# Where the norm weights are applied: on the features or on the weight matrices

## The chip, the cores and the metric

One core of one Trainium2 chip. The metric is the device time in microseconds (us) of one execution. The kernel before was timed three times: 1508.42, 1510.27 and 1512.3 us, median 1510.27.

## What is computed

A sequence of 256 rows of width 1024 goes through two blocks in fp32. What matters here is that every projection is preceded by a norm with a weight vector `g`, and that the product is linear in both:

```python
def rmsnorm(x, g):
    xf = x.astype(jnp.float32)
    y = xf * lax.rsqrt(jnp.mean(xf * xf, axis=-1, keepdims=True) + NORM_EPS)
    return y.astype(x.dtype) * g
...
    for l in range(DEPTH):
        g = norm_gains[l]
        h = rmsnorm(x, g[0])
        if l % 2 == 0:
            y = even_mixer(h, ...)
        else:
            y = odd_mixer(h, ...)
        x = x + rmsnorm(y, g[1])
        h = rmsnorm(x, g[2])
        x = x + rmsnorm(memory_cross_attention(h, mem_n, w_q[l], w_kv[l], w_o[l]), g[3])
        h = rmsnorm(x, g[4])
        x = x + rmsnorm(squared_relu_mlp(h, w_ff1[l], w_ff2[l]), g[5])
```

The second block is a differential attention, an MLP, an S5 state space layer (`ssm`) and an MLP, each behind a norm with its own weights; the attention's heads go through another norm (`subln`) before `w_o`. Per layer of the first block there are a mixer (pooling and a gated recurrence in layer 0, banded attention in layer 1), attention to a normed memory `mem`, and an MLP. The MLPs are 1024 to 4096 to 1024.

## The kernel before

Every fp32 product is made as three matmuls of fp32r parts: each operand is split into a high part (a rounded copy) and a low part (the value less the high part), and hi x hi, hi x lo and lo x hi are summed. The rows stand in two tiles of 128 (`X`, t = 0 and 1). The row factor of a norm is applied after the product, the weight vector `g` before it.

*Activations.* `feat_half` (L133 to L144) transposes four 128x128 blocks of `X` on TensorE (L140) into one PSUM tile `tp`, copies it to `hh` on ACT (L143) and makes `hl` = tp - hh on DVE (L144), 128x512 each. Two halves make one row tile's features. `residual` (L178) puts these calls into a list, `later`, that `now` (L206) runs in the midst of the next product. `mem_feat` (L407) does the same once for the memory (`mh`, `ml`), after a sum of squares on ACT (L416) and a scaling on DVE (L421).

*Weights.* A `Seg` (L25) is a panel of a weight matrix. `_load` (L34) fetches 512 KB at a time into a `raw` buffer (four of them) by a transfer that SP issues (L42), ACT makes `whi`, DVE `wlo` (rings of ten). One `raw` holds one k tile of 128x1024, or two of 128x512. Where a weight vector belongs to the rows of the matrix, its column of `gcols` (or `sg`, for `subln`) is the scale, k tile by k tile:

```python
            if self.gain is None:
                nc.scalar.activation(out=hi, in_=src, func=AF.Copy)                       # L47
                ...
            else:
                for a, kt in enumerate(kts):
                    g = self.gain[:, kt:kt + 1]
                    nc.scalar.activation(out=hi[:, a], in_=src[:, a], func=AF.Copy, scale=g)  # L53
                    ...
                        nc.vector.scalar_tensor_tensor(out=lo[:, a], in0=src[:, a], scalar=g, ...)  # L58
```

*Products.* `proj_b` (L259) has the weights stationary and gives feature-major results (`pb`, 128x256 matmuls, L224 to L226), `proj_a` (L242) the activations stationary (`pacc`, `acc`, 128x512, L217 to L219). `mlp` (L275) works in eight chunks of 512 hidden columns, `ffps` and `ffacc`. The second layer's MLP of the first block and the first MLP of the second block also run `tables` between their matmuls, a generator that makes the S5 layer's tables: `er`, `gr`, `cmt`, `bb` on DVE (L1149 to L1157, L1376), `bm` partly on GpSimd, transposes `etp` on TensorE (L1402) and copies `eo` and `kl` on ACT (L1403, L1416). `diff` (L628) is the differential attention.

*Order.* A scheduler fixes the order of the instructions on each engine when the program is built; each engine then runs its list strictly in that order. In `even` (L858) a block under `manual_schedule` (L889) makes the first features and the first panel. SP issues the transfers in its own list: `X`, `gcols` (L1825), the first weights, some small tables, `mem` (L413).

Of the kernel before, what the change touches and what calls it, by code (L numbers as in the profile page):

```python
# [24 lines left out]
class Seg:  # L25


    def __init__(self, c, dram, c0, width, kts, gain=None, share=False):
# [4 lines left out]

    def _load(self, i):  # L34
# [5 lines left out]
        for j in range(2):  # L40
# [5 lines left out]
            if self.gain is None:  # L46
                nc.scalar.activation(out=hi, in_=src, func=AF.Copy)  # L47
                eng = nc.gpsimd if self.share and j else nc.vector
                eng.tensor_tensor(out=lo, in0=src, in1=hi.bitcast(F32), op=ALU.subtract)  # L49
# [19 lines left out]
class Core:  # L69
# [108 lines left out]
    def residual(self, t, acc, gain=None, rsq=None, feat=True, rows=True):  # L178
# [16 lines left out]
        for q in range(2):  # L195
# [1685 lines left out]
```

## Time and profile before

| what | value |
|---|---|
| median of three runs | 1510.27 us |
| the profiled execution | 1508.71 us |
| its span from the first instruction to the last | 1506.9 us |
| TensorE (PE) busy | 1426.2 us, 95% |
| VectorE (DVE) busy | 1129.7 us, 75% |
| ScalarE (ACT) busy | 835.0 us, 55% |
| GpSimd (POOL) busy | 184.0 us, 12% |
| DMA, mean | 198 GB/s |

The profile is one execution. Its views used here: groups of instructions by line (how often, how long), waits (who stood still, for whom), busy time by stretch of the span, and the timeline. A wait is idle time of an engine that ended with the named event. Idle time of an engine that nobody waits for costs nothing. `PEclk` is TensorE's granted clock as a share of its full speed.

### The profile page before, as it was taken

What the parts mean: (1) busy time and instruction counts of PE and PEld (TensorE: products, weight loads), DVE (VectorE), ACT (ScalarE), POOL (GpSimd) and SP (SyncE); (2) the same over time, 40 slices, a digit from 0 to 9 for tenths busy, and PEclk for the clock granted to TensorE, in tenths of its full rate; (3) what the DMA queues carried; (4) which work ended last, traced back from release to release, by engine and by line L of the source; (5) the groups of instructions that cost most, each with busy time, mean ns of one, the idle gap of its engine ahead of it and who ended that gap; (6) DMA issues with size and microseconds to landing.
All of it is one profiled execution on the core that took longest, in us unless ns stands there. A gap on an engine that the chain in (4) does not pass through costs nothing. (4 is left out here: it accounts for less than half of the span.)

```text
span 1506.9 us, 25499 instructions
## 1 busy us (share of the span) xinstructions
PE 1426.2 (95%) x9668; PEld 1239.6 (82%) x9668; DVE 1129.7 (75%) x2013; ACT 835.0 (55%) x1432; POOL 184.0 (12%) x206
## 2 busy tenths in 40 slices
PE   8999999999999999989899999999999968999997
PEld 8897888998789798869778877888879756889895
DVE  7986658997776866579995699899995587674651
ACT  7475546454464665556445667665454555564540
POOL 1241001000000000023440010123430000000000
PEclk9999999999999999999999999999999998999999
DMA  8464535475785455365768663347668887655640
GB/s 298 145 206 155 188 119 188 152 238 181 241 284 188 127 182 194 114 210 191 232 211 255 210 219 114 111 146 235 220 223 265 319 315 274 198 184 192 206 158 28
DMA packets 134034, 298.26 MB, mean 198 GB/s; under 512 B 16152, under 2 KB 36376, under 8 KB 133272
## 3 DMA queue, kind: packets, MB, share of 16 engines
q1 hardware_dynamic: 133624, 294.54, 58.9%
q0 software_dynamic: 288, 2.10, 0.4%
q8 instruction: 76, 1.25, 0.3%
q14 instruction: 46, 0.38, 0.1%
HBM read 270.15 MB, written 31.62 MB: 200 GB/s over the span
## 5 line engine op out<-in xcount | busy, mean ns | idle before, releaser
L58 DVE SCALAR_TENSOR_TENSOR wlo<-raw,gcols,whi 128x512 fp32r<-128x512 f32 (+1 forms) x456 | 356.7, 825 | 66.5 <-ACT whi L53 66.3
L53 ACT ACTIVATE whi<-raw,gcols 128x512 fp32r<-128x512 f32 (+1 forms) x456 | 316.7, 745 | 128.0 <-DMA raw<-in_w_ff 27.4
L49 DVE TENSOR_TENSOR wlo<-raw,whi 128x1024 fp32r<-128x1024 f32 x172 | 206.7, 1220 | 65.1 <-ACT whi L47 64.6
L47 ACT ACTIVATE whi<-raw 128x1024 fp32r<-128x1024 f32 x176 | 181.8, 1054 | 99.1 <-DMA raw<-in_ffn_w_down 28.6
L224 PE MATMUL ffps<-hh,whi 128*128 128x256 f32 x768 | 222.0, 289 | 0.2 <-ACT kl L1416 0.2
L226 PE MATMUL ffps<-hl,whi 128*128 128x256 f32 x768 | 219.6, 286 | 0.0
L225 PE MATMUL ffps<-hh,wlo 128*128 128x256 f32 x768 | 219.4, 286 | 0.0
L217 PE MATMUL ffacc<-whi,ah 128*128 128x512 f32 x512 | 206.1, 403 | 2.3 <-ACT whi L47 2.3
L218 PE MATMUL ffacc<-wlo,ah 128*128 128x512 f32 x512 | 203.5, 397 | 0.7 <-DVE wlo L49 0.7
L219 PE MATMUL ffacc<-whi,al 128*128 128x512 f32 x512 | 203.4, 397 | 0.0
L224 PEld LDWEIGHTS ffps<-hh,whi 128*128 128x128 f32 x768 | 148.2, 193 | 2.4 <-issue 1.4
L225 PEld LDWEIGHTS ffps<-hh,wlo 128*128 128x128 f32 x768 | 147.8, 192 | 0.5
L226 PEld LDWEIGHTS ffps<-hl,whi 128*128 128x128 f32 x768 | 147.6, 192 | 0.0
L217 PEld LDWEIGHTS ffacc<-whi,ah 128*128 128x128 f32 x512 | 97.3, 190 | 25.5 <-ACT whi L47 2.7
L218 PEld LDWEIGHTS ffacc<-wlo,ah 128*128 128x128 f32 x512 | 97.5, 190 | 22.7 <-DVE wlo L49 1.6
L219 PEld LDWEIGHTS ffacc<-whi,al 128*128 128x128 f32 x512 | 97.2, 190 | 23.0
L225 PE MATMUL pb<-hh,wlo 128*128 128x256 f32 x352 | 101.1, 289 | 2.9 <-DVE wlo L58 2.9
L224 PE MATMUL pb<-hh,whi 128*128 128x256 f32 x352 | 101.3, 290 | 2.2 <-ACT whi L53 2.2
L226 PE MATMUL pb<-hl,whi 128*128 128x256 f32 x352 | 100.8, 287 | 0.0
L171 POOL TENSOR_TENSOR r<-r,mhalf 128x1 f32<-128x1 f32 x32 | 24.7, 771 | 563.9 <-DVE r L170 557.2
L299 DVE TENSOR_TENSOR relu<-relu 128x512 f32<-128x512 f32 x64 | 45.7, 714 | 58.2 <-ACT relu L298 58.0
L298 ACT ACTIVATE relu<-ffps 128x512 f32<-128x512 f32 x64 | 43.9, 685 | 76.0 <-PE ffps L226 61.6
(481 smaller groups left out, 3001.7 us busy)
## 6 DMA issues: line engine op xcount, KB each, us to landing
raw<-in_w_ff SPq DMA_DIRECT2D x128, 512.0 KB, 4.6
raw<-in_ffn_w_up SPq DMA_DIRECT2D x64, 512.0 KB, 4.5
raw<-in_ffn_w_down SPq DMA_DIRECT2D x64, 512.0 KB, 4.4
raw<-in_w_mem_kv SPq DMA_DIRECT2D x32, 512.0 KB, 4.8
raw<-in_w_qkv SPq DMA_DIRECT2D x24, 512.0 KB, 4.9
raw<-in_attn_w_qkv SPq DMA_DIRECT2D x24, 512.0 KB, 4.7
raw<-in_w_in_ab SPq DMA_DIRECT2D x20, 512.0 KB, 5.1
raw<-in_w_mem_q SPq DMA_DIRECT2D x16, 512.0 KB, 5.1
```

What stands on the lines that cost most here:

```text
L47: nc.scalar.activation(out=hi, in_=src, func=AF.Copy)
L49: eng.tensor_tensor(out=lo, in0=src, in1=hi.bitcast(F32), op=ALU.subtract)
L53: nc.scalar.activation(out=hi[:, a], in_=src[:, a], func=AF.Copy, scale=g)
L58: nc.vector.scalar_tensor_tensor(out=lo[:, a], in0=src[:, a], scalar=g, in1=hi[:, a].bitcast(F32), op0=ALU.mult, op1=ALU.subtract)
L217: nc.tensor.matmul(o, xh, wh[:, s], start=first, stop=False)
L218: nc.tensor.matmul(o, xh, wl[:, s], start=False, stop=False)
L219: nc.tensor.matmul(o, xl, wh[:, s], start=False, stop=last)
L224: nc.tensor.matmul(out, wh, xh, start=first, stop=False)
L225: nc.tensor.matmul(out, wl, xh, start=False, stop=False)
L226: nc.tensor.matmul(out, wh, xl, start=False, stop=last)
L298: nc.scalar.activation(out=o, in_=ps if view is None else ps.rearrange("p (f c j) -> p f c j", f=2, j=8), func=AF.Relu)
L299: nc.vector.tensor_tensor(out=r, in0=r, in1=r, op=ALU.mult)
```

## The change

The vectors scale the activations. `feat_half` takes a `gain`: with a matrix of columns (128x8), each of its four 128x128 blocks has its own scale, so the ACT copy and the DVE subtraction are made block by block; with one column (128x1, `sg`) they stay 128x512. The 40 halves that go into normed products (36 `hh`, 4 `mh`) become four and four operations; the 4 halves of `diff`'s `o` keep one and one. All weights are split unscaled, one 128x1024 operation on ACT and one on DVE for each raw, except the first two raws of the first panel (`fine=1`), which stay in 128x512 pieces. The counts of transfers and of matmuls are the same. Matrices that had a gain: 244 raws, 212 of them in two 128x512 pieces, 32 in one 128x1024; 8 more of `w_o` had `sg`.

```diff
@@ class Seg, _load
-            if self.gain is None:
-                nc.scalar.activation(out=hi, in_=src, func=AF.Copy)
-                eng = nc.gpsimd if self.share and j else nc.vector
-                eng.tensor_tensor(out=lo, in0=src, in1=hi.bitcast(F32), op=ALU.subtract)
-            else:
-                for a, kt in enumerate(kts):
-                    g = self.gain[:, kt:kt + 1]
-                    nc.scalar.activation(out=hi[:, a], in_=src[:, a], func=AF.Copy, scale=g)
...
-                        nc.vector.scalar_tensor_tensor(out=lo[:, a], in0=src[:, a], scalar=g, in1=hi[:, a].bitcast(F32),
-                                                       op0=ALU.mult, op1=ALU.subtract)
+            eng = nc.gpsimd if self.share and j else nc.vector
+            for s in [slice(a, a + 1) for a in range(h)] if i < self.fine else [slice(0, h)]:
+                nc.scalar.activation(out=hi[:, s], in_=src[:, s], func=AF.Copy)
+                eng.tensor_tensor(out=lo[:, s], in0=src[:, s], in1=hi[:, s].bitcast(F32), op=ALU.subtract)
@@ feat_half
-        h = hi[:, ks, :]
-        nc.scalar.activation(out=h, in_=t3, func=AF.Copy)
-        nc.vector.tensor_tensor(out=lo[:, ks, :], in0=t3, in1=h.bitcast(F32), op=ALU.subtract)
+        h, l = hi[:, ks, :], lo[:, ks, :]
+        for s in (slice(0, 4),) if gain.shape[1] == 1 else (slice(j, j + 1) for j in range(4)):
+            g = gain if gain.shape[1] == 1 else gain[:, 4 * q + s.start:4 * q + s.stop]
+            nc.scalar.activation(out=h[:, s], in_=t3[:, s], func=AF.Copy, scale=g)
+            nc.vector.scalar_tensor_tensor(out=l[:, s], in0=t3[:, s], scalar=g, in1=h[:, s].bitcast(F32), op0=ALU.mult, op1=ALU.subtract)
@@ even
-                self.to_feat(self.X[:, t], hh[:, t], hl[:, t])
-            proj(1024, decay)
+                self.to_feat(self.X[:, t], hh[:, t], hl[:, t], gain)
+            proj(1024, decay, 1)
@@ residual: the next norm's columns come in as feat
-                self.later.append(lambda q=q: self.feat_half(X, q, self.hh[:, t], self.hl[:, t]))
+                self.later.append(lambda q=q: self.feat_half(X, q, self.hh[:, t], self.hl[:, t], gain=feat))
```

The other lines hand the columns to `residual`, `mem_feat` and `ssm` in place of the products, and make `sg` 128x1.

The scheduler orders the changed instructions anew. Three places, as the order of the two programs prints them. First ACT at the start: the features of `X` (`hh`), the first weights (`whi`), the memory's sum of squares (`ml,mms<-mem`). Before:

```order
L143 ACTIVATE hh_88<-tp_138 128x512
L143 ACTIVATE hh_88<-tp_145 128x512
L53 ACTIVATE whi_155<-raw_153,gcols_109 128x512 x2
L53 ACTIVATE whi_163<-raw_161,gcols_109 128x512 x2
L53 ACTIVATE whi_183<-raw_181,gcols_109 128x512 x2
L53 ACTIVATE whi_191<-raw_189,gcols_109 128x512 x2
L168 ACTIVATE junk_233,ms_234<-X_90 128x512 x2
```

After (the first seven slices of `hh` stand ahead of these rows):

```order
L899 ACTIVATE lbe_335<-lbe_335 128x4
L137 ACTIVATE hh_88<-tp_137,gcols_109 128x128
L137 ACTIVATE hh_88<-tp_150,gcols_109 128x128 x3
L410 ACTIVATE ml_115,mms_642<-mem_638 128x1024
L137 ACTIVATE hh_88<-tp_150,gcols_109 128x128
L137 ACTIVATE hh_88<-tp_163,gcols_109 128x128 x4
L49 ACTIVATE whi_179<-raw_177 128x512 x2
L49 ACTIVATE whi_187<-raw_185 128x512 x2
L49 ACTIVATE whi_207<-raw_205 128x1024
L49 ACTIVATE whi_213<-raw_211 128x1024
```

The sum of squares of the memory and the recurrence's `lbe` stand now ahead of the first weight split; the sum of squares stood behind sixteen of them before. In the list of SP, which is not printed, the second gain vector `gB`, `d_rows`, `g_rows` and two more small tables now come right behind the first half of `mem`, ahead of the fifth weight transfer; DVE multiplies `d_rows` by `g_rows` two slices before its first weight split.

Second, DVE in the even mixer, between the first panels' splits (`wlo`), the decay chain (`x`, `lx`, `f`, and `b`, the scan) and the memory's scaling (`mem`). Before:

```order
L939 SCALAR_TENSOR_TENSOR x_119<-x_119,lx_340 128x1024
L938 TENSOR_TENSOR f_342<-f_342,ls_352 128x1024
L874 TENSOR_TENSOR u0_360<-pb_444,rb_121 128x2x256
L943 SCALAR_TENSOR_TENSOR b_358<-reset_327,f_342 128x1024
L58 SCALAR_TENSOR_TENSOR wlo_534<-raw_531,gcols_109,whi_533 128x512 x2
L421 TENSOR_SCALAR mem_634<-mem_634,r_643 128x512
```

After:

```order
L922 SCALAR_TENSOR_TENSOR lx<-x 128x1024
L868 TENSOR_TENSOR u_380<-pb,rb 128x2x256
L415 TENSOR_SCALAR mem<-mem,r 128x512 x4
L50 TENSOR_TENSOR wlo<-raw,whi 128x1024
L931 SCALAR_TENSOR_TENSOR ls<-x,lx 128x1024
L933 SCALAR_TENSOR_TENSOR x<-x,lx 128x1024
L932 TENSOR_TENSOR f<-f,ls 128x1024
L868 TENSOR_TENSOR u_380<-pb,rb 128x2x256
L937 SCALAR_TENSOR_TENSOR b<-reset,f 128x1024
L960 TENSOR_TENSOR w<-u_380 128x4x256
L50 TENSOR_TENSOR wlo<-raw,whi 128x1024
```

Before, the last two pieces of the third panel stood behind the scan; now all splits of the first three panels stand ahead of these rows (two of them just ahead of `x`), the memory's scaling and one further split go before the chain.

Third, DVE in a chunk of the first table stage: four `wlo` of the second MLP matrix have been made (the last of them is the first L49 or L50 row), then the next chunk's first matrix. Before:

```order
L49 TENSOR_TENSOR wlo<-raw,whi 128x1024
L1376 TENSOR_TENSOR bb<-bb,gb 128x128
L49 TENSOR_TENSOR wlo<-raw,whi 128x1024
L58 SCALAR_TENSOR_TENSOR wlo<-raw,gcols,whi 128x512
L1151 TENSOR_TENSOR er<-pk,bb 128x512
L1152 TENSOR_TENSOR er<-pk,bb 128x512
L1153 TENSOR_TENSOR er<-er,cmt 128x512
L1157 TENSOR_TENSOR er<-er,cmt_8104 128x512
L58 SCALAR_TENSOR_TENSOR wlo<-raw,gcols,whi 128x512
L1151 TENSOR_TENSOR gr<-pk,bc 128x4x128
L1417 SCALAR_TENSOR_TENSOR kl<-dmask,d_rows,kl 128x16
```

After:

```order
L50 TENSOR_TENSOR wlo<-raw,whi 128x1024
L1370 TENSOR_TENSOR bb<-bb,gb 128x128
L50 TENSOR_TENSOR wlo<-raw,whi 128x1024
L1145 TENSOR_TENSOR er<-pk,bb 128x512
L1146 TENSOR_TENSOR er<-pk,bb 128x512
L1147 TENSOR_TENSOR er<-er,cmt 128x512
L1151 TENSOR_TENSOR er<-er,cmt_8052 128x512
L50 TENSOR_TENSOR wlo<-raw,whi 128x1024 x2
L1411 SCALAR_TENSOR_TENSOR kl<-dmask,d_rows,kl 128x16
L1145 TENSOR_TENSOR gr<-pk,bc 128x4x128
L1146 TENSOR_TENSOR gr<-pk,bc 128x4x128
L1147 TENSOR_TENSOR gr<-gr,cmt 128x4x128
```

The first two raws' `wlo` stand together behind the four `er` operations, one operation for each; before, the first piece stood ahead of them and the second behind.

## Rows read from the trace of the kernel before

**Rows 1.** The page's part 1: busy us, share of the span, instructions.

```profile
PE 1426.2 (95%) x9668; PEld 1239.6 (82%) x9668; DVE 1129.7 (75%) x2013; ACT 835.0 (55%) x1432; POOL 184.0 (12%) x206
```

**Rows 2.** Groups by line and shape, whole span (line, tiles, count | busy, mean ns | idle).

```profile
L58 DVE SCALAR_TENSOR_TENSOR wlo<-raw,gcols,whi 128x512 fp32r<-128x512 f32 x424 | 313.9, 784 | 59.1 <-ACT whi L53 58.9
L53 ACT ACTIVATE whi<-raw,gcols 128x512 fp32r<-128x512 f32 x424 | 280.8, 715 | 114.5 <-DMA raw<-in_w_ff 27.4 <-DMA raw<-in_ffn_w_up 23.6 <-PE ffacc L219 12.3
L49 DVE TENSOR_TENSOR wlo<-raw,whi 128x1024 fp32r<-128x1024 f32 x172 | 206.7, 1220 | 65.1 <-ACT whi L47 64.6
L47 ACT ACTIVATE whi<-raw 128x1024 fp32r<-128x1024 f32 x176 | 181.8, 1054 | 99.1 <-DMA raw<-in_ffn_w_down 28.6 <-DMA raw<-in_w_ff 27.8 <-PE pb L226 20.6
L144 DVE TENSOR_TENSOR hl<-tp,hh 128x512 fp32r<-128x512 f32 x36 | 23.4, 683 | 2.2 <-ACT hh L143 2.2
L143 ACT ACTIVATE hh<-tp 128x512 fp32r<-128x512 f32 x36 | 19.6, 586 | 4.2 <-PE tp L140 4.1
L1416 ACT ACTIVATE kl<-klag 128x144 f32<-128x144 f32 x16 | 4.3, 270 | 0.0
```

**Rows 3.** Busy time by stretch: engines (instructions), PEclk, DMA share, GB/s.

```profile
690.00:800.00 110.00, 100.22 (x813) 87.15 (x815) 105.35 (x166) 59.46 (x105) 39.73 (x36) 0.95 0.68 225
870.00:980.00 110.00, 105.05 (x565) 84.10 (x563) 101.74 (x245) 77.41 (x161) 11.61 (x8) 1.00 0.45 145
880.00:890.00 10.00, 10.00 (x45) 8.04 (x44) 10.00 (x11) 6.96 (x12) 2.96 (x1) 1.00 0.64 215
1025.00:1135.00 110.00, 103.51 (x839) 91.11 (x837) 103.92 (x164) 57.75 (x111) 40.59 (x38) 0.97 0.67 224
```

**Rows 4.** Waits, 690 to 800 us (first three), then 1025 to 1135 us.

```profile
PE etp L1402 <- ACT eo L1403: 5.6, 2, 3.3
ACT whi L53 <- DMA raw<-in_w_ff: 17.4, 4, 5.9
DVE wlo L58 <- ACT whi L53: 2.2, 4, 0.8
...
DVE wlo L58 <- ACT whi L53: 3.0, 6, 0.8
```

**Rows 5.** Timeline, runs of equal operations (start, us, engine, line, xcount).

```profile
321.10 2.73 DVE L58 SCALAR_TENSOR_TENSOR wlo<-raw,gcols,whi 128x512 fp32r<-128x512 f32 x4
324.49 2.35 DVE L49 TENSOR_TENSOR wlo<-raw,whi 128x1024 fp32r<-128x1024 f32 x2
331.95 1.41 DVE L58 SCALAR_TENSOR_TENSOR wlo<-raw,gcols,whi 128x512 fp32r<-128x512 f32 x2
...
318.60 2.55 ACT L53 ACTIVATE whi<-raw,gcols 128x512 fp32r<-128x512 f32 x4
321.54 2.00 ACT L47 ACTIVATE whi<-raw 128x1024 fp32r<-128x1024 f32 x2
330.32 1.34 ACT L53 ACTIVATE whi<-raw,gcols 128x512 fp32r<-128x512 f32 x2 [0.88 <-DMA raw<-in_w_ff]
...
123.52 1.12 DVE L1107 SCALAR_TENSOR_TENSOR y<-o,r,og 128x128 f32<-128x128 f32 x4 [0.91 <-POOL r L123]
...
L1107 DVE SCALAR_TENSOR_TENSOR y<-o,r,og x8: 341/343/351, 123.5 to 133.0; 128x128 f32<-128x128 f32 x8
```

**Rows 6.** The start: timeline of ACT, PE and SP, and tile mem.

```profile
7.67 0.60 ACT L143 ACTIVATE hh<-tp 128x512 fp32r<-128x512 f32 x1 [0.35 <-PE tp L140]
9.09 5.32 ACT L53 ACTIVATE whi<-raw,gcols 128x512 fp32r<-128x512 f32 x8 [0.82 <-DMA raw<-in_w_in_ab]
...
9.86 0.79 PE L224 MATMUL pb<-hh,whi 128*128 128x256 f32 x2 [2.23 <-ACT whi L53]
...
10.36 0.33 SPq L413 DMA_DIRECT2D mem<-in_mem  x1
...
L416 ACT ACTIVATE ml<-mem x2: 1047/1050/1052, 24.4 to 25.7; 128x1024 fp32r<-128x1024 f32 x2
DMA to landing us min/median/max: 6.4/6.4/6.4
...
raw<-in_w_in_ab SPq DMA_DIRECT2D x20, 512.0 KB, 5.1
```

**Rows 7.** Timeline at 38 to 42 us, and busy time by stretch.

```profile
37.98 2.28 DVE L943 TENSOR_TENSOR_SCAN b<-reset,f 128x1024 f32<-128x1024 f32 x1
40.17 2.17 DVE L58 SCALAR_TENSOR_TENSOR wlo<-raw,gcols,whi 128x512 fp32r<-128x512 f32 x2
...
40.95 0.58 PE L225 MATMUL pb<-hh,wlo 128*128 128x256 f32 x1 [2.86 <-DVE wlo L58]
...
20.00:30.00 10.00, 10.00 (x87) 10.00 (x86) 9.66 (x20) 9.79 (x19) 0.56 (x1) 1.00 0.84 285
40.00:50.00 10.00, 9.05 (x52) 8.96 (x53) 10.00 (x13) 3.83 (x4) 5.22 (x5) 0.66 0.18 53
70.00:120.00 50.00, 50.00 (x361) 46.87 (x360) 40.63 (x50) 37.81 (x61) 20.56 (x10) 1.00 0.60 200
```

**Rows 8.** Timeline of DVE in the first table stage; its splits, 690 to 800 us.

```profile
750.60 0.68 DVE L1151 TENSOR_TENSOR er<-pk,bb 128x512 f32<-128x512 f32 x1
754.48 1.55 DVE L1151 TENSOR_TENSOR gr<-pk,bc 128x512 f32<-128x512 f32 x1
...
L58 DVE SCALAR_TENSOR_TENSOR wlo<-raw,gcols,whi 128x512 fp32r<-128x512 f32 x32 | 29.0, 949 | 2.2 <-ACT whi L53 2.2
```

**Rows 9.** Waits, 870 to 980 us.

```profile
PE acc L217 <- ACT hh L143: 0.3, 1, 0.3
```

More of the change, by code (lines that the diff above doesn't have):

```diff
@@ L176, in row_scale, with residual @@
         self.r[t] = self.rms([self.X[:, t, j * 512:j * 512 + 512] for j in range(2)], tag=f"rx{t}_", bufs=2)
-    def residual(self, t, acc, gain=None, rsq=None, feat=True, rows=True):
+    def residual(self, t, acc, gain=None, rsq=None, feat=None, rows=True):
         nc = self.nc
@@ L240, in feat32, with proj_a @@
             nc.scalar.activation(out=dst[:, 4 * q:4 * q + 4, :], in_=t.rearrange("p (k n) -> p k n", k=4), func=AF.Copy)
-    def proj_a(self, hh, hl, w, c0, done, gain=None, turns=((0, 0, 8), (1, 0, 8)), step=None, share=False, now=(0, 3)):
-        seg = Seg(self, w, c0, D, range(KT), gain, share)
+    def proj_a(self, hh, hl, w, c0, done, turns=((0, 0, 8), (1, 0, 8)), step=None, share=False, now=(0, 3)):
+        seg = Seg(self, w, c0, D, range(KT), share)
         a = [None, None]
@@ L257, in proj_a, with proj_b @@
                 step()
-    def proj_b(self, hh, hl, w, c0, consume, gain=None, groups=4):
+    def proj_b(self, hh, hl, w, c0, consume, groups=4, fine=0):
         seg = None
@@ L263, in proj_b @@
             if g % 2 == 0:
-                seg = Seg(self, w, c0 + g * 256, 512, range(KT), gain)
+                seg = Seg(self, w, c0 + g * 256, 512, range(KT), fine=0 if g else fine)
             ps = self.ps.tile([128, 2, 256], F32, tag="ps", name="pb")
@@ L273, in proj_b, with mlp @@
             consume(g, ps)
-    def mlp(self, pool, w1, gain, w2, done, perm=False, fill=None):
+    def mlp(self, pool, w1, w2, done, perm=False, fill=None):
         nc = self.nc
@@ L361, in mlp @@
         parts = {c: parts_tiles() for c in range(2)}
-        segs = [Seg(self, w1, ch * 512, 512, range(KT), gain) for ch in range(2)]
+        segs = [Seg(self, w1, ch * 512, 512, range(KT)) for ch in range(2)]
         last = None
@@ L404, with mem_feat @@
 class Attn:
-    def mem_feat(self, parts, mem):
+    def mem_feat(self, parts, mem, gain):
         nc = self.nc
@@ L475, in put_feat, with cross @@
         self.nc.vector.tensor_tensor(out=ol[:, :, ks, :].rearrange("p t k n -> p k t n"), in0=src, in1=h.bitcast(F32), op=ALU.subtract)
-    def cross(self, pool, w_q, gain, kv, out, w_o, done):
+    def cross(self, pool, w_q, kv, out, w_o, done):
         nc = self.nc
@@ L527, in head @@
                 values(h - 2)
-        self.proj_b(self.hh, self.hl, w_q, 0, head, gain)
+        self.proj_b(self.hh, self.hl, w_q, 0, head)
         scores(3)
@@ L533, in cross, with band @@
         self.proj_a(oh, ol, w_o, 0, done, turns=TAIL)
-    def band(self, pool, w_qkv, gain, relb, w_o, done):
+    def band(self, pool, w_qkv, relb, w_o, done):
         nc = self.nc
@@ L626, in band, with diff @@
         self.proj_a(oh, ol, w_o, 0, done, turns=TAIL)
-    def diff(self, pool, w_qkv, gain, q_gain, k_gain, lam_vecs, subln, w_o, cos2, sin2, done):
+    def diff(self, pool, w_qkv, q_gain, k_gain, lam_vecs, subln, w_o, cos2, sin2, done):
         nc = self.nc
@@ L847, in diff @@
         self.later += values(1)
-        self.proj_a(Halves(oh), Halves(ol), w_o, 0, done, sg, turns=HALF, now=(1, 2))
+        self.proj_a(Halves(oh), Halves(ol), w_o, 0, done, turns=HALF, now=(1, 2))
 LAM0 = 0.8 - 0.6
@@ L1086, in even @@
         step()
-        self.proj_a(hh, hl, w_in, 1536, vg, gain, turns=HALF, step=step)
+        self.proj_a(hh, hl, w_in, 1536, vg, turns=HALF, step=step)
         mem_keys(step)
@@ L1477, in load_phases, with ssm @@
         self.tbs[b] = t
-    def ssm(self, pool, X, w_glu):
+    def ssm(self, pool, X, w_glu, gain):
         nc = self.nc
@@ L1723, in first_block @@
         g = A["norm_gains"][l]
-        gc = [c.gcols[:, 3 * l + i, :] for i in range(3)]
+        gc = [c.gcols[:, 3 * l + i, :] for i in range(3)] + [c.gcols[:, 7 if l else 3, :]]
         side = tc.tile_pool(name=f"kv{l}", bufs=1, side="right", reuse_waits="tile")
```

77 lines of the change are left out of this document (37 added, 40 removed).

## The prediction

> **What bounds the kernel now.** I read the page's totals first: TensorE (PE) is busy 95% of 1506.9 us, VectorE (DVE) 75%, ScalarE (ACT) 55% [rows 1]. So work taken from DVE or ACT is worth nothing by itself; it counts only in stages where PE waits for them. The costliest DVE and ACT groups are what the change touches: the weight splits with a gain, 424 pairs of 128x512 operations beside 172 splits without a gain in 128x1024 [rows 2]. Then I read the stages. In 690 to 800 and 1025 to 1135 us (the two MLPs that also fill in the S5 tables) DVE is busy 105.35 and 103.92 of 110 us and PE only 100.22 and 103.51; in 870 to 980 us (diff attention) DVE has 101.74, PE 105.05 [rows 3]. These are the stages with something to win. In the waits of the first table stage PE stands 5.6 us before the transposes `etp` for ACT's copy `eo`, ACT 17.4 us for weight transfers, while DVE hardly waits at all (2.2 us, for `whi`) [rows 4]. A transfer starts when DVE has read the raw buffer it overwrites, so the late transfers are DVE's lateness seen from ACT: the sum is made on DVE's time there. Last I read the start, because the order of instructions moves there most.
>
> **Sizes.** A gained raw of 512 KB is two ops on each engine before, one after. DVE: four 128x512 in a row take 2.73 us, two 1.41, so one each 0.66 us and 1.32 per raw; two 128x1024 take 2.35 where one is busy 1.22, so 1.13 per raw [rows 2, 5]. 0.19 us saved; 212 raws give 40 us of DVE work. ACT: 2.55 for four, 1.34 for two, so 0.605 each and 1.21 per raw, against 2.00 minus 1.05 = 0.95 [rows 2, 5]: 0.26 saved, 55 us in all. The other side: 40 feature halves, one op of 0.683 on DVE and 0.586 on ACT before [rows 2], become four 128x128 ops. No row shows the scaled form from PSUM; the nearest are a 128x128 of the same DVE operation, 0.343 us alone and four in a row in 1.12 [rows 5], and ACT's `kl` (128x144, from PSUM) at 0.270 us [rows 2]. Bounds on DVE: 1.12 back to back to 4 x 0.343 = 1.37 one by one, so +0.44 to +0.69 a half, 18 to 28 us; ACT between four overlapping (about 0.8, +0.2) and 1.08 (+0.5), 8 to 20 us. I take the low end on DVE, since the four stand in a row. DVE gains some 22 us net, ACT some 40, nearly all of it where PE is the bound and nothing comes of it. The eight `w_o` raws lose their gain too: already 128x1024, they keep one operation on each engine and count as nothing.
>
> The Trainium skill ("VectorE: DVE Perf Modes", the section on the TRN2 errata) speaks against the slices: a fixed latency per instruction is paid by every small tile, and tiles of at least 512 elements are advised. By its formulas a half from PSUM would go from 658 to 1033 ns on DVE: +0.38 by estimate, beside my +0.44 from rows. The sum would be the same by it; the rule turns the sign only if the slices lie on PE's path, which rival B below prices.
>
> **1. The start: +5 us (bounds +3 to +10).** Before, the last of four `hh` copies ends at 8.27 us, ACT gets the first weight at 9.09 and PE begins its first matmul at 9.86 [rows 6]. In the new order ACT runs eleven slices and then the Square of `mem` (L416 before, L410 after); five slices and all weight splits stand behind it. `mem` is issued at 10.36 and lands 6.4 us later [rows 6], so at 16.75. Its issue depends on raw transfers before it, which do not move. ACT runs strictly in order, so: 16.75 + 1.05 (Square) + 5 slices of about 0.27 (1.35) + 0.7 (first `whi`) = 19.85 us for the first matmul, 10 later than before. DVE has `d_rows` in the same place, which waits for `g_rows`, a small transfer issued three after `mem`; it should be done by 19 and hide behind ACT. The raws 4 to 7 need the slots of 0 to 3, now freed from about 21 us; they land 5.1 us after their issue (the median [rows 6]) and are split by 32, when PE is about to end the 96 matmuls of raws 0 to 3 (11 us at 87 in 10 us [rows 7], some 13 with the slow first ones). So the delay does not grow. Part comes back: before, PE stood 2.86 us at 40.95 for `wlo`, which DVE made only after the 2.28 us scan, and its granted clock over 40 to 50 us was 0.66 [rows 7]: a mean between the levels of 1.2 and 2.4 GHz, after 2.86 us without a matmul. At 1.0 that window would hold up to 3.4 us more of work, the wait included in part. In the new order all weight splits of the first three segments stand ahead of the scan and PE, being 10 us late, finds them ready: minus 3 for the wait, minus 2 for the clock. If none comes back: +10.
>
> **2. The two table stages: -10 us (bounds -16 to -3).** 32 gained raws lie there (64 ops). Size alone: 32 x 0.19 = 6.1 us. DVE's idle time before `wlo`, 2.2 and 3.0 us [rows 4], goes in part: where DVE came to `wlo` too early and waited, it now does the four `er` operations first; I take 4 of the 5.2. The `wlo` there cost 29.0 us for 32, not 32 x 0.66 = 21.1, and an ordinary 128x512 op of one line takes 1.55 us at 754.48 against 0.68 at 750.60 [rows 8]: when GpSimd is at work, DVE operations stretch. I let those 8 us per stage stand, as GpSimd's work is unchanged. The ceiling is PE's own lost time, 9.8 + 6.5 = 16.3 us; the floor, half of the size alone (-3).
>
> **3. Diff attention: -3 us (0 to -5).** DVE is the busy engine, PE's loss is 4.95 us [rows 3]. 24 raws x 0.19 = 4.6, less about 1 for the slices. A few `hh` slices now stand behind key-side copies on ACT; their lead on PE is short.
>
> **4. Slices at the norm boundaries: +1 us (0 to +3).** Nine times the features of the next product are made. Two halves add 0.8 to 1.4 us to DVE. PE meanwhile runs the other row tile's matmuls: three k tiles of six 128x512 each, at 45 in 10 us [rows 3] about 4 us, which covers it; without that cover it is up to 9 us.
>
> **5. All else: 0.** The other MLPs and cross attentions run at PE's pace; the S5 stage is bound by chains that the change does not touch; DMA counts and matmuls are equal.
>
> **Sum.** +5 - 10 - 3 + 1 = -7 us. Against the profiled execution's own 1508.71 us that is 1501.7; the median of the runs, 1510.27, lies 1.56 above it, so I forecast **1503**. A measurement of this kernel can tell about 0.3%, 4.5 us, from no change.
>
> **Rivals.**
> *A, slower: the head of the queue at the start.* ACT's wait for `mem` costs the full 10 us and nothing is returned, because PE has no slack after it: it is busy all 50 us from 70 to 120 [rows 7]. The tables give their size alone (-6.1), since the transfers, not DVE, turn out to pace the raws; diff gives nothing, slices +1. 10 - 6.1 + 1 = +4.9: **1515.2**. It decides once stages 2 and 3 and the start's return together bring under 6.5 us. For it: the order is certain, and the landing of `mem` has a row. Against: the clock and the wait at 40 us.
> *B, no change.* The slices lie on the path, at the nine boundaries and in diff: +0.8 each, 7 us in place of my +1. -7 + 6 = -1: **1509**. Against it: PE has other matmuls to run there, and at its boundaries before it stood for `hh` only 0.3 us in the diff stage [rows 9]. The Trainium skill's rule on small tiles, named above, speaks for it.
> *C, larger gain.* The tables reach PE's pace: DVE is behind PE by only 5 to 10 us in each stage, and with its idle time, the copies `eo` and the clock (0.95 and 0.97 granted [rows 3], worth 5.5 and 3.3 us) all 16.3 us and some 4 of clock come back. +5 - 20 - 3 + 1 = -17: **1493**. For it: the waits on `eo` are a consequence of DVE's lateness. Against: GpSimd's stretching stays.
> *D, the change doesn't do what it says.* Not so: the order shows the 128x1024 ops. But the scheduler's order, not the sizes, may carry the result; that is in A and C.
>
> The Trainium skill ("Trainium Architecture — The Big Picture", on SBUF's two sides) calls the port that DVE shares with GpSimd an exclusive lock. The stretched rows above agree in kind; by that rule the held time would not shrink with fewer DVE operations, as I assumed.
>
> **Chances.** Forecast (gains of 5 to 13 us) 0.40, C 0.15, B 0.25, A 0.20. So faster by over 0.3%: 0.55; within: 0.25; slower: 0.20. Range: 1492 (C, with diff at its bound) to 1516 (A).
>
> **What would show it.** At the start: the first weight split on ACT at about 19 us, behind the Square, and PE's first `pb` matmul near 19.9. At 40 to 60 us: no wait of PE for `wlo` behind the scan, clock 1.0. Each table stage some 5 us shorter in all, DVE without idle time before `wlo`, 128x1024 splits near 1.22 us. Slices: about 0.34 us each on DVE and 0.27 on ACT. I am wrong if the first matmul comes before 15 us, if DVE in the table stages is no longer the busy engine, or if PE waits for `hh` or `hl` at the boundaries by more than 3 us in sum.

## The result: 1.3% slower

The changed kernel took 1529.17 us (median of 4 runs, 1526.48 to 1532.52) against 1509.35 us of the kernel before (4 runs, 1507.75 to 1512.3): a ratio of 1.013, with an interval of 1.010 to 1.016. The forecast was 1503 us, with a range of 1492 to 1516. The profiled execution, the slowest of the four, took 1532.52 us with a span of 1530.6.

The page of the changed kernel, part 1, then two groups of part 5:

```profile
PE 1432.2 (94%) x9668; PEld 1241.5 (81%) x9668; DVE 1119.2 (73%) x1923; ACT 802.1 (52%) x1342; POOL 193.9 (13%) x206
...
L50 DVE TENSOR_TENSOR wlo<-raw,whi 128x1024 fp32r<-128x1024 f32 (+1 forms) x426 | 532.3, 1267 | 157.7 <-ACT whi L49 156.1
L49 ACT ACTIVATE whi<-raw 128x1024 fp32r<-128x1024 f32 (+1 forms) x430 | 442.9, 1051 | 235.4 <-DMA raw<-in_w_ff 50.0
```

The work did shrink beside [rows 1, 2]: ACT from 835.0 to 802.1 us, DVE from 1129.7 to 1119.2. The time went the other way, so it went into waits. The first place is the start. ACT's timeline there, with one row of DVE (L898):

```profile
7.46 0.37 ACT L137 ACTIVATE hh<-tp,gcols 128x128 fp32r<-128x128 f32 x1 [5.43 <-DMA gcols<-in_gcols]
8.24 0.37 ACT L137 ACTIVATE hh<-tp,gcols 128x128 fp32r<-128x128 f32 x1 [0.42 <-DVE hl L138]
9.03 0.37 ACT L137 ACTIVATE hh<-tp,gcols 128x128 fp32r<-128x128 f32 x1 [0.42 <-DVE hl L138]
...
14.86 0.16 DVE L898 TENSOR_TENSOR lbe<-lbl 128x4 f32<-128x4 f32 x1 [3.25 <-DMA lbl<-in_rec_lb_logits]
15.06 0.20 ACT L899 ACTIVATE lbe<-lbe 128x4 f32<-128x4 f32 x1 [3.05 <-DVE lbe L898]
...
17.48 1.05 ACT L410 ACTIVATE ml<-mem 128x1024 fp32r<-128x1024 f32 x1
...
21.39 4.08 ACT L49 ACTIVATE whi<-raw 128x512 fp32r<-128x512 f32 x6
```

A slice starts 0.78 to 0.79 us after the one before it, though it lasts 0.37: ACT stands 0.42 us until DVE's subtraction of the slice before is done. The Square of `mem` (17.48 us), which the prediction feared, waits for nothing when its turn comes. `lbe`, which the new order also puts among the slices, does wait: ACT stands 3.05 us for DVE, and DVE for the small transfer `lbl`. The first weight is split at 21.39 us, and PE follows:

```profile
22.06 0.80 PE L218 MATMUL pb<-hh,whi 128*128 128x256 f32 x2 [13.55 <-ACT whi L49]
```

That is 12.2 us later than in [rows 6]. From the first slice to the first weight ACT needs 13.9 us: 9.6 for the sixteen slices with their waits, 3.3 for `lbe` and 1.0 for the Square. Over the whole span, the changed kernel's line 137 (ACT's slices), first what ACT stood idle for, then who waited for it (us, times):

```profile
L137 ACT ACTIVATE hh<-tp,gcols x144: 346/363/401, 7.5 to 1346.6; 128x128 fp32r<-128x128 f32 x144
...
  DVE hl L138: 13.6, 33
...
  DVE hl L138: 14.3, 28
...
  PE ffps L211: 2.5, 3
```

For 144 slices ACT stood 33 times for DVE and DVE 28 times for ACT; away from the start, other work often fills the turn. The program itself says why. ACT's first instructions of the changed kernel, with the counters that each waits for (`DVE_49` counts DVE's instructions, `PE_49` PE's, `DMAHW4_49` is the transfer of `gcols`):

```
2 L137 ACTIVATE hh<-tp,gcols 128x128 [waits DMAHW4_49,PE_49]
3 L137 ACTIVATE hh<-tp,gcols 128x128 [waits DVE_49] x3
4 L137 ACTIVATE hh<-tp,gcols 128x128 [waits PE_49]
```

The first slice of a half waits for PE's transposes, each later one for DVE: ACT's copy and DVE's subtraction read the same PSUM tile `tp`, and the program lets only one of them at it at a time (s5 below, where only `tp` is divided, rules out the other shared tiles, `hh` and `hl`). With one operation per half there was one such hand-over; with slices written copy, subtraction, copy, subtraction there are seven. The Trainium skill ("PSUM — Partial Sum Buffer", section "PSUM bank collisions raise a hardware error") says that two engines may not access one bank over the same partitions at once, two reads included, and that the software must keep them apart by bank and not by address. The waits here agree: the program makes the slices wait though they touch different columns.

Where the rest arose is read by comparing the start of the same group of matmuls on PE in two profiled executions. In the table each number is that start minus the one in the kernel before, in us; the kernels other than the changed one are the experiments below.

| before at | place on PE | changed | s1 | s2 | s4 | s5 | s9 | s10 |
|---|---|---|---|---|---|---|---|---|
| 9.9 | first matmul | +12.2 | +1.3 | +0.3 | +12.5 | +3.4 | -0.5 | -0.3 |
| 446.9 | band begins | +13.0 | -0.3 | -5.3 | +9.5 | +5.6 | -0.1 | -3.4 |
| 659.1 | first table MLP | +18.5 | +4.0 | -2.4 | +10.2 | +8.7 | +0.9 | -3.7 |
| 799.6 | its last table | +18.6 | +5.8 | -2.5 | +9.5 | +4.6 | -11.8 | -4.9 |
| 1007.6 | diff ends | +26.2 | +8.9 | +1.1 | +13.5 | +11.0 | -11.5 | -4.7 |
| 1135.1 | last table | +25.1 | +12.0 | +0.8 | +15.5 | +6.3 | -16.3 | -4.4 |
| 1337.8 | last MLP | +23.7 | +7.8 | -1.6 | +14.3 | +6.8 | -18.9 | -3.4 |

The changed kernel loses 12.2 us at the start, 5.5 between the band and the tables and 7.6 in diff attention, and gains nothing in the tables. A column is one execution: s10 leaves everything behind the band as it was, and its differences there still run from -3.4 to -4.9. A step of 1 or 2 us in a column therefore says nothing.

### The profile page after: what moved, and what is told of

The parts are those of the page before. It is cut to its first block, busy times and chain, and to the rows that moved or that the text cites. A ratio compares the mean times of both kernels' runs of the same rounds, so it can differ in the third digit from the quotient of the medians.

```text
span 1530.6 us, 25337 instructions
## 1 busy us (share of the span) xinstructions
PE 1432.2 (94%) x9668; PEld 1241.5 (81%) x9668; DVE 1119.2 (73%) x1923; ACT 802.1 (52%) x1342; POOL 193.9 (13%) x206
## 5 line engine op out<-in xcount | busy, mean ns | idle before, releaser
L50 DVE TENSOR_TENSOR wlo<-raw,whi 128x1024 fp32r<-128x1024 f32 (+1 forms) x426 | 532.3, 1267 | 157.7 <-ACT whi L49 156.1
L49 ACT ACTIVATE whi<-raw 128x1024 fp32r<-128x1024 f32 (+1 forms) x430 | 442.9, 1051 | 235.4 <-DMA raw<-in_w_ff 50.0
L218 PE MATMUL pb<-hh,whi 128*128 128x256 f32 x352 | 100.5, 286 | 13.6 <-ACT whi L49 13.6
L165 POOL TENSOR_TENSOR r<-r,mhalf 128x1 f32<-128x1 f32 x32 | 27.8, 870 | 598.7 <-DVE r L164 598.7
L218 PEld LDWEIGHTS pb<-hh,whi 128*128 128x128 f32 x352 | 67.1, 191 | 14.4 <-ACT whi L49 14.0
L286 ACT ACTIVATE ah<-relu 128x512 fp32r<-128x512 f32 x48 | 30.4, 633 | 84.3 <-DVE relu L293 84.3
```

The lines of the kernel that those rows point to most:

```text
L49: nc.scalar.activation(out=hi[:, s], in_=src[:, s], func=AF.Copy)
L50: eng.tensor_tensor(out=lo[:, s], in0=src[:, s], in1=hi[:, s].bitcast(F32), op=ALU.subtract)
L165: nc.gpsimd.tensor_tensor(out=r, in0=r, in1=self.mhalf[:, 0:1], op=ALU.pow)
L218: nc.tensor.matmul(out, wh, xh, start=first, stop=False)
L286: nc.scalar.activation(out=out[0], in_=src, func=AF.Copy)
```

## The experiments

**s1_grouped: the four copies ahead of the four subtractions.** Against the changed kernel:

```diff
+        for s, g in zip(ss, gs):
             nc.scalar.activation(out=h[:, s], in_=t3[:, s], func=AF.Copy, scale=g)
+        for s, g in zip(ss, gs):
             nc.vector.scalar_tensor_tensor(out=l[:, s], in0=t3[:, s], scalar=g, ...)
```

> The same 128x128 operations, but the four copies on ACT are written ahead of the four subtractions on DVE, so each half hands its PSUM tile over once and not seven times. Theory H (the hand-over: both engines read the same PSUM tile `tp`, each slice waits for the other engine's slice before it, and other work slips in between): ACT's waits on `hl` (13.6 us) vanish, the first product begins near 12.5 us instead of 22.06 (gcols at 7.4, sixteen slices of 0.27, one split), the boundaries lose their +2 us each, total 1510 to 1515. Rival N (the number of small operations costs, not their order): the start improves only as far as the memory's sum of squares moves back, the boundaries and the diff stage keep their +11 us, total 1517 to 1521.

Measured 1517.44 us, 1.0052 (interval 1.0037 to 1.0067) of the kernel before, which had 1507.98 in that job. The start is as theory H had it, but the total lies just above H's range, in that of rival N. ACT and PE at the start of this kernel:

```profile
6.34 4.23 ACT L138 ACTIVATE hh<-tp,gcols 128x128 fp32r<-128x128 f32 x16 [4.31 <-DMA gcols<-in_gcols]
10.35 4.19 ACT L49 ACTIVATE whi<-raw 128x512 fp32r<-128x512 f32 x6
...
18.64 0.19 ACT L901 ACTIVATE lbe<-lbe 128x4 f32<-128x4 f32 x1
...
11.14 0.80 PE L220 MATMUL pb<-hh,whi 128*128 128x256 f32 x2 [3.67 <-ACT whi L49]
```

The sixteen slices are one run of 4.23 us, 0.26 each, as the prediction had them, and PE begins 10.9 us earlier. Of these, 5.6 us are the slices (4.0 for 9.6 up to the first weight) and 4.3 come from the scheduler, which now puts `lbe` and the Square behind the first weights; some 1.1 us are no merit of the edit: the `gcols` transfer landed earlier in this execution (first slice at 6.34, not 7.46). One hand-over per half, with the order that the scheduler then makes, is worth 0.78% of the time. What is left is still slower than before.

**s2_oneop: one 128x512 operation per half, scaled by the first column alone.**

```diff
-        for s in (slice(0, 4),) if gain.shape[1] == 1 else (slice(j, j + 1) for j in range(4)):
...
+        g = gain[:, 0:1]
+        nc.scalar.activation(out=h, in_=t3, func=AF.Copy, scale=g)
+        nc.vector.scalar_tensor_tensor(out=l, in0=t3, scalar=g, in1=h.bitcast(F32), op0=ALU.mult, op1=ALU.subtract)
```

> The weights as in the change; the features scaled in one 128x512 operation per half on each engine by the first column of the gains alone, so the other three blocks of each half get a wrong gain (the output is not the reference's). This is the change without its slices. Theory H and rival N both: 1503 to 1508, the first product near 10.5 us (9.86 plus the wait for gcols). Rival W (the unscaled 128x1024 weight splits, by their size and the order that follows, are what costs in the later stages): the diff stage still loses 5 us or more, total 1513 to 1520.

Measured 1509.66 us, 1.0008 [0.9993, 1.0022] (10 runs), a little above the expected 1508. So the 128x1024 splits without any slices bring nothing in total that can be told from zero: of 5.3 us won by the band (the table), most are lost again behind it. Beside s1 it prices the number of slices: 7.8 us, without the alternation.

**s3_bcast: one multiplication of `tp` in place, by columns broadcast along the row, then copy and subtraction of 128x512.**

```diff
+        nc.vector.tensor_tensor(out=t3, in0=t3, in1=gain[:, 4 * q:4 * q + 4].unsqueeze(2).to_broadcast([128, 4, 128]), op=ALU.mult)
+        nc.scalar.activation(out=h, in_=t3, func=AF.Copy)
+        nc.vector.tensor_tensor(out=l, in0=t3, in1=h.bitcast(F32), op=ALU.subtract)
```

> DVE multiplies `tp` in place by the four gain columns (one 128x512 operation with a broadcast operand), then ACT copies and DVE subtracts in 128x512 as before the change: one operation of about 0.75 us more per half on DVE than before, one hand-over more. Theory H: start near 11 to 12 us (each half 0.75 + 0.6 + 0.7 in a chain, halves overlapping), boundaries about +0.7 us each against before, total 1506 to 1512. Rival N: three operations instead of eight, 1506 to 1512 as well; it tells which form is the better repair. Rival W: 1515 or more.

Measured 1521.25 us, 1.0075 [1.0051, 1.0098], far over the 1506 to 1512 of theories H and N. DVE at its start:

```profile
6.94 0.70 DVE L139 TENSOR_TENSOR tp<-tp,gcols 128x512 f32<-128x512 f32 x1 [2.68 <-DMA gcols<-in_gcols]
8.30 0.69 DVE L141 TENSOR_TENSOR hl<-tp,hh 128x512 fp32r<-128x512 f32 x1 [0.66 <-ACT hh L140]
8.91 0.69 DVE L139 TENSOR_TENSOR tp<-tp,gcols 128x512 f32<-128x512 f32 x1
```

Few operations, but again a chain through one tile: multiply, ACT's copy, subtract, 1.97 us a half. The first matmul comes at 16.91 us, 7.0 later than before; what makes the rest of its loss was not looked into.

**s4_fineall: all weights unscaled, but in the former 128x512 pieces.**

```diff
-            for s in [slice(a, a + 1) for a in range(h)] if i < self.fine else [slice(0, h)]:
+            for s in [slice(a, a + 1) for a in range(h)]:
```

> The change with all weights split unscaled but in the pieces of 128x512 that they had before (where the matrix is 512 wide). Theory H and rival N: the sizes of the weight splits matter only in the table stages; those lose the 1 to 3 us that they won, the rest stays, total 1528 to 1535. Rival W: the order that comes with the 128x1024 pieces is the cause, total 1515 or less.

Measured 1522.22 us, 1.0083 [1.0068, 1.0098], between the two expected ranges: smaller weight pieces make the change cheaper by nearly half a per cent, which is seen behind the start (the table above: 9.5 against 13.0 at the band, 10.2 against 18.5 at the tables). Between the band and the tables the change loses 5.5 us, s1 and s2, which also have the whole pieces, 4.2 and 3.0, and s4 0.8: there the whole pieces seem to cost, whatever the slices. How pieces and slices meet shows on ACT at a boundary, the first MLP's features. The changed kernel:

```profile
242.50 0.35 ACT L137 ACTIVATE hh<-tp,gcols 128x128 fp32r<-128x128 f32 x1
242.75 1.05 ACT L49 ACTIVATE whi<-raw 128x1024 fp32r<-128x1024 f32 x1
243.70 0.61 ACT L137 ACTIVATE hh<-tp,gcols 128x128 fp32r<-128x128 f32 x2
244.19 1.06 ACT L49 ACTIVATE whi<-raw 128x1024 fp32r<-128x1024 f32 x1
245.82 0.37 ACT L137 ACTIVATE hh<-tp,gcols 128x128 fp32r<-128x128 f32 x1 [0.56 <-DVE hl L138]
246.09 1.05 ACT L49 ACTIVATE whi<-raw 128x1024 fp32r<-128x1024 f32 x1
247.04 0.36 ACT L137 ACTIVATE hh<-tp,gcols 128x128 fp32r<-128x128 f32 x1
...
248.60 0.61 ACT L137 ACTIVATE hh<-tp,gcols 128x128 fp32r<-128x128 f32 x2
...
250.24 0.39 ACT L137 ACTIVATE hh<-tp,gcols 128x128 fp32r<-128x128 f32 x1
```

The kernel before and s1 at the same place:

```profile
230.27 1.06 ACT L143 ACTIVATE hh<-tp 128x512 fp32r<-128x512 f32 x2
```

```profile
233.54 2.16 ACT L138 ACTIVATE hh<-tp,gcols 128x128 fp32r<-128x128 f32 x8
```

Two halves take 1.06 us before, 2.16 as eight grouped slices, and 8.1 us (242.50 to 250.63) in the changed kernel: between two slices, while DVE has its turn, the list puts a weight split of 1.05 us. Those splits are work that has to be done, and PE stood only 0.6 us for `hh` at this boundary.

**s5_banks: slices written as in the change, each 128x128 block in a PSUM tile of its own.**

```diff
+            t = self.ps.tile([128, 1, 128], F32, tag="ps", name="tp")
+            nc.tensor.transpose(t[:, 0], src[:, k * 128:(k + 1) * 128], self.ident)
...
+            nc.scalar.activation(out=h[:, s], in_=t, func=AF.Copy, scale=g)
+            nc.vector.scalar_tensor_tensor(out=l[:, s], in0=t, scalar=g, in1=h[:, s].bitcast(F32), op0=ALU.mult, op1=ALU.subtract)
```

> The change with the slices in their own order (copy, subtraction, copy, subtraction), but each 128x128 block transposed into a PSUM tile of its own, so that ACT and DVE never read the same one: no slice waits for the other engine's slice before it, the operations are the same. The memory's sum of squares moves back behind the first weights of itself. Theory H (hand-over of the shared PSUM tile): like the grouped form, first product at 11 to 12 us, total 1514 to 1519, unless the four PSUM buffers, all taken by one half, make TensorE wait. Rival N (the number or the interleaving of small operations): 1524 or more.

Measured 1515.38 us, 1.0054 [1.0034, 1.0073] (10 runs; before 1507.54 in that job). ACT and PE at its start, then the longest of PE's waits (us, times, longest):

```profile
7.55 1.14 ACT L148 ACTIVATE hh<-tp,gcols 128x128 fp32r<-128x128 f32 x4 [5.52 <-DMA gcols<-in_gcols]
...
13.22 0.80 PE L229 MATMUL pb<-hh,whi 128*128 128x256 f32 x2 [0.97 <-ACT whi L49]
```

```profile
PE tp L143 <- DVE hl L149: 13.5, 13, 3.7
```

The operations and the order in which they are written are the change's; only the shared tile is gone, and with it the alternation: four slices in 1.14 us. So the shared tile makes the alternation. The scheduler's order changes with it: as in s1, `lbe` and the Square come behind the first weights. The price is the last row: four PSUM tiles for each half run out, and PE waits 13.5 us for one to come free.

**s6_order: the change, with the memory's load and Square at a low priority, so that they stand behind the first weights.**

```diff
+        with self.low(400):
+            m = [self.sb.tile([128, D], F32, tag=n, name="mem") for n in ("y", "junk")]
...
+            r = self.rstd(ms, 2, tag="mr")
```

> The change as it is, the memory's load and sum of squares given a lower priority, so that they come behind the first weights; `lbe` still stands among the slices. It parts the two causes at the start. Theory H: the slices' alternation and `lbe` make most of the +12.2 us, the sum of squares 1 to 2 us: first product at 20 to 21 us, total 1526 to 1529. Rival Q (the head of the queue, as the prediction had it): first product at 13 us or before, total 1520 or less.

Measured 1530.24 us, 1.0154 [1.0111, 1.0197]. ACT's first slice and `lbe`, and PE's first matmul:

```profile
6.45 0.37 ACT L137 ACTIVATE hh<-tp,gcols 128x128 fp32r<-128x128 f32 x1 [4.43 <-DMA gcols<-in_gcols]
...
13.76 0.20 ACT L900 ACTIVATE lbe<-lbe 128x4 f32<-128x4 f32 x1 [2.76 <-DVE lbe L899]
...
20.25 0.79 PE L218 MATMUL pb<-hh,whi 128*128 128x256 f32 x2 [12.82 <-ACT whi L49]
```

Of 12.2 us only 1.8 come back, 1.0 of them because `gcols` landed earlier here (6.45 for 7.46), and none in the total. The load and Square of `mem`, on which the prediction's first term rests, are not what held the start. `lbe` still does, by 2.76 us; a form of the change that moves it too was not run, and its share in the total is not measured by itself.

**s7_grpfine: s1, with the band's keys and queries and diff attention's weights split in 128x512 pieces.**

```diff
-        self.proj_b(self.hh, self.hl, w_qkv, D, keys)
+        self.proj_b(self.hh, self.hl, w_qkv, D, keys, fine=2)
...
-            seg = Seg(self, w_qkv, c0, 512, range(KT))
+            seg = Seg(self, w_qkv, c0, 512, range(KT), fine=2)
```

> The grouped form, with the weights of the band attention's keys and queries and of the diff attention split unscaled in 128x512 pieces. In the two forms with coarse pieces and cheap features these stages lost 2 and 3 us. Theory C (coarse pieces are what costs there: a 1.2 us operation ahead of a chain of short ones on DVE): the grouped form's total less 3 to 5 us, 1512 to 1515. Rival (the slices cost there, and the pieces nothing): 1517 as the grouped form.

Measured 1511.81 us, 1.0028 [1.0006, 1.0050] (10 runs). The total is 5.6 us under s1's, in another job, as theory C had it; but by PE's starts, diff attention costs 2.5 us here and 3.0 in s1, and the difference arises elsewhere (2.8 us are won between 659 and 800 us of the kernel before, where s1 loses 1.9). So the coarse pieces of these matrices are not shown to be what diff loses by.

**s8_hybrid: s7, with the gain left on the weights for the input projection and the memory's keys and values.**

```diff
+        if gain is None:
+            nc.scalar.activation(out=h, in_=t3, func=AF.Copy)
+            nc.vector.tensor_tensor(out=l, in0=t3, in1=h.bitcast(F32), op=ALU.subtract)
+            return
```

> As the last one, but the first matrix and the memory's matrices keep their gain on the weights, as before the change, so the first features and the memory's are plain. It takes away the start's +2.3 us and the memory's +0.8. Theory H with C: 1508 to 1512, no faster than the kernel before; if the features of the later boundaries cost less than the unscaled weights win (5.7 us by the end of the band attention's start, 3 us in the S5 stage), 1503 to 1507, and it beats both.

Measured 1505.72 us, 0.9997 [0.9977, 1.0017] (10 runs): no slices at the start, and the loss is gone, but nothing is gained that can be told from zero, though the total lies in the range that stood for a gain (1503 to 1507).

**s9_nolo: the kernel before, with `wlo` of the first matrix left out in the two table MLPs.**

```diff
-            lo = c.ring.tile([128, h, w], F32R, tag="lo", name="wlo")
+            lo = hi if self.nolo else c.ring.tile([128, h, w], F32R, tag="lo", name="wlo")
...
+                    if self.nolo:
+                        continue
```

> The kernel before, with the `wlo` subtraction of the first MLP matrix left out in the two MLPs that fill in the tables (the high part is used in its place; the output is not the reference's). It takes 64 operations of 128x512, some 29 us, off DVE in each table stage and leaves the matmuls, the transfers and ACT as they are. It asks what DVE's time is worth there. Theory D (the prediction's step: DVE's busy time sets the pace, so what DVE saves PE gets back up to its own loss): 8 us or more faster in the two stages together, total 1492 to 1500. Rival P (the pace is set by the chain of `er`, `gr`, `cmt` and `klag` through DVE, GpSimd and ACT in the order that the scheduler gives, and by ACT's copies `eo` behind weights not yet there): 3 us or less, total 1505 to 1508.

Measured 1486.66 us, 0.9858 [0.9831, 0.9885], more than theory D expected (1492 to 1500). Busy time in its two table stages (columns as in [rows 3]):

```profile
688.00:798.00 110.00, 110.00 (x943) 97.79 (x943) 87.23 (x137) 67.45 (x117) 38.55 (x37) 1.00 0.78 260
...
1020.00:1130.00 110.00, 110.00 (x943) 97.75 (x942) 81.53 (x126) 62.58 (x117) 39.84 (x36) 1.00 0.77 252
```

Without the [rows 8] group of 29.0 us, PE is busy all the time at full clock, and the run is 22 us shorter. DVE's part did bound these stages, as the prediction read it; whether by its time, by the `raw` buffers that it holds until it has read them, or by the `wlo` buffers, this run doesn't part. The change in the same stages:

```profile
709.00:819.00 110.00, 99.38 (x822) 86.19 (x820) 104.74 (x149) 57.04 (x93) 40.91 (x36) 0.97 0.71 235
1050.80:1160.80 110.00, 104.74 (x871) 92.16 (x869) 106.31 (x150) 54.04 (x96) 41.69 (x37) 0.97 0.70 228
```

DVE is as full as before, 104.74 for 105.35 and 106.31 for 103.92. DVE's groups in the first of these stretches (and of the kernel before in 690 to 800 us, below):

```profile
L50 DVE TENSOR_TENSOR wlo<-raw,whi 128x1024 fp32r<-128x1024 f32 x33 | 46.7, 1433 | 4.3 <-ACT whi L49 4.3
L1146 DVE TENSOR_TENSOR er<-pk,bb 128x512 f32<-128x512 f32 x6 | 7.6, 1259 | 0.0
L287 DVE TENSOR_TENSOR al<-relu,ah 128x512 fp32r<-128x512 f32 x8 | 7.2, 901 | 0.7 <-ACT ah L286 0.7
```

```profile
L49 DVE TENSOR_TENSOR wlo<-raw,whi 128x1024 fp32r<-128x1024 f32 x16 | 19.2, 1214 | 0.7 <-ACT whi L47 0.7
...
L293 DVE TENSOR_TENSOR al<-relu,ah 128x512 fp32r<-128x512 f32 x8 | 5.5, 683 | 0.7 <-ACT ah L292 0.7
...
L1152 DVE TENSOR_TENSOR er<-pk,bb 128x512 f32<-128x512 f32 x6 | 5.0, 826 | 0.0
```

The size term came: 32 raws cost 29.0 + 19.2 = 48.2 us before, 33 cost 46.7 now, 2.9 us less for the same number. But other operations grew: `al` from 5.5 to 7.2 us, the second `er` from 5.0 to 7.6, by the stretch that the prediction ascribed to GpSimd. And DVE's idle time before `wlo` did not fall but rose, from 2.9 (2.2 + 0.7) to 4.3.

**s10_ffband: the kernel before, with the features scaled only for the first MLP and the band.** Copies and subtractions are grouped; these two steps split their weights unscaled, the band's keys and queries in 128x512 pieces.

```diff
+        for j in range(4):
+            nc.scalar.activation(out=h[:, j:j + 1], in_=t3[:, j:j + 1], func=AF.Copy, scale=gs[j])
+        for j in range(4):
+            nc.vector.scalar_tensor_tensor(out=l[:, j:j + 1], in0=t3[:, j:j + 1], scalar=gs[j], ...)
...
-                c.band(pool, A["w_qkv"], gc[0], A["rel_bias"], A["w_o_att"], done)
+                c.band(pool, A["w_qkv"], None, A["rel_bias"], A["w_o_att"], done)
```

> The kernel before, with the vectors moved to the features in two products alone: the first MLP and the band attention of layer 1 (grouped slices, keys and queries in 128x512 pieces, all else as before). In the hybrid form the span from 245 to 447 us is where the change wins, 5 us, and later stages give it back. If the win stays where it is: 1502 to 1506, faster than both kernels. Rival: the win comes from elsewhere or is lost again in the reordered stages behind it: 1506 to 1511.

Measured 1504.02 us (12 runs), 0.9973 [0.9959, 0.9986], the kernel before at 1508.63 in that job: 4.6 us faster than it, so it beats both. By PE's starts 3.4 us are won ahead of the band, and the rest is within the noise of one execution. PE's wait there, before (400 to 450 us) and in s10 (398 to 448):

```profile
PE tp L140 <- DVE X L200: 3.3, 1, 3.3
```

```profile
PE tp L144 <- DVE X L211: 0.5, 1, 0.5
```

## Why the prediction was wrong

**The step that failed is "Sizes", and with it the first and the fourth term: the wait of each slice for the other engine stood at nothing.** It priced a slice as an operation by its own duration, "four 128x128 ops" back to back, and took for granted that ACT's next copy runs while DVE subtracts. The durations were right (ACT 363 ns and DVE 346 at the median, one by one; 0.26 in a row in s1). What was missing is the wait between them, which made 0.785 us of each slice at the start. Comparing ratios to the kernel before, each within its own job, the loss falls into three parts:

- the hand-over and the order that the scheduler made of it, the change against s1: 1.0130 - 1.0052, 0.8% or about 12 us. Nothing of it was in the prediction. Most of it is the start: 5.6 us of slices and 4.3 of `lbe` and the Square;
- four small operations in place of one, s1 against s2: 0.44%, some 7 us (7.8 by the medians). The prediction had +1 for it and rival B +7, which was the right size in part by luck: B put it at the boundaries and in diff, and diff shows none of it (3.0 us lost in s1, 3.6 in s2). The Trainium skill's rule on small tiles, cited for B ("VectorE: DVE Perf Modes", the TRN2 errata), agrees as far as that: at the start s1's sixteen slices take ACT 4.23 us, s2's four operations 2.42;
- the rest, s2 against before: 0.08%, not distinct from zero. Here the prediction had the -13 us of tables and diff.

**Term 1, the start (+5).** The first matmul was forecast at 19.85 and came at 22.06, which looks near and is not: the sum made it out of the wait for `mem`, which did not occur, and 0.27 us a slice, which was 0.785, and it had no price for `lbe`, which cost 3.3. `mem` was issued at 11.03 us and landed some 6 us later, so by estimate quick slices in the same order would have waited for it, as the sum said; the slow ones hid that wait. s6 took the Square away and won 1.8 us; s1 and s5 took the alternation away, and with it `lbe` and the Square, and began at 11.14 and 13.22. The return of 5 us did not come: +12.2 at the first matmul, +13.0 at the band. The wait behind the scan was gone and the clock was 1.00 from 40 to 60 us, as foreseen, but PE met the next wait of the same chain (PE's timeline and the stretch 60 to 70 us, changed kernel):

```profile
65.65 1.12 PE L132 MATMUL tp<-ident,mem 128*128 128x128 f32 x4 [5.10 <-DVE q L948]
```

```profile
60.00:70.00 10.00, 4.90 (x16) 3.70 (x16) 9.27 (x26) 6.34 (x16) 1.20 (x1) 0.69 0.17 55
```

5.10 us in place of 2.86, and the granted clock 0.69 in place of 0.66 [rows 7]: the gap was moved, not closed. The sum subtracted a wait and did not ask which part of the same chain comes late next.

**Term 2, the tables (-10).** Measured 0.1 later in the first stage and 1.1 earlier in the second (the table of PE's starts), so nothing that can be told from zero. The reading was right that DVE paces PE there (s9), and the 3 us a stage of size came. DVE's rows of the first stage show what stands against them: 4.3 us more on `al` and the second `er`, and 1.4 more of waiting for `whi`; the step "where DVE came to `wlo` too early and waited, it now does the four `er` operations first" did not hold. s5, with the same weight splits in another order, won 4.1 and 4.8 us in the two stages, and s1 lost 1.9 and 3.2: by single executions, the order is worth as much here as the sizes. Which order is good, and why, these runs don't show.

**Term 3, diff attention (-3).** The changed kernel loses 7.6 us there, s1 3.0, s2 3.6. DVE's busy time over the stretch of [rows 3] did fall, while PE kept its own and lost clock:

```profile
890.00:1000.00 110.00, 105.11 (x541) 84.38 (x542) 96.82 (x229) 70.35 (x145) 10.96 (x6) 0.95 0.42 135
```

96.82 for 101.74 on DVE, PE 105.11 for 105.05, the clock 0.95 for 1.00. So less work on the busiest engine did not help PE. Some 4.6 us are the hand-over (the change against s1); the other 3.0 are left with s1, and 3.6 with s2, which has no slices, so neither the slices nor the hand-over makes them. Their cause stays open.

**Term 4, the boundaries (+1).** The condition in the prediction was "PE waits for `hh` or `hl` at the boundaries by more than 3 us in sum": 2.5 us for `hh` and 1.7 for `hl` before line 211 alone, where it stood 0.3 before [rows 9].

**Rival A** had the right sign, and one half of it held: nothing of the start's loss came back. Its cause did not hold: s6 takes the load and Square of `mem` away, and the loss stays. Of the head of the queue only `lbe`, which A did not name, held the start. The rival that was missing is one step of the program wide: which engine's instruction releases the next one.

## What to carry to other kernels

Before one operation is cut into n, ask what each piece waits for: two engines that read one PSUM tile in turn hand it over at every piece (0.785 us a slice here, for 0.26 in a row), so write all pieces of one engine first, or give each piece its own tile if there are enough. A change of sizes is worth trying step by step, since the same edit gained at one place (s10, 4.6 us in all) and lost at others. Every operation that the new order puts ahead of the first weight needs a price, the small ones too (`lbe`: 0.2 us of work, 3.05 of waiting). And where the sum subtracts a stall, name the wait that comes behind it in the same chain.

## What was not expected of the hardware

The program keeps two engines' reads of one PSUM tile apart even where their columns differ: 33 waits of ACT for DVE, 13.6 us, and 28 the other way, 14.3 us; with a tile for each block, four copies ran in 1.14 us. DVE's 128x1024 subtraction takes 1.22 us at the median of the changed kernel and up to 2.94. DVE in the first table stage of s2:

```profile
747.71 4.09 DVE L50 TENSOR_TENSOR wlo<-raw,whi 128x1024 fp32r<-128x1024 f32 x2
...
768.83 2.35 DVE L50 TENSOR_TENSOR wlo<-raw,whi 128x1024 fp32r<-128x1024 f32 x2
```

The same pair takes 4.09 us where it falls on GpSimd's work (`cmt`, two of 1.45 and 2.04 us from 747.26 us on) and 2.35 elsewhere. So what a table stage gains by a larger operation may depend on where the order puts it; no run here shows that by itself.
